# A conv FFN in fp32 halves on one core: down projection by token halves and groups of four inner tiles in the buffers of the up projection, and three plain column pairs instead of two

## The chip, the cores and the metric

The kernel runs on one core of a Trainium2 chip. The metric is the device time of the program in microseconds (us), the median over runs. TensorE (PE in the rows) multiplies, VectorE (DVE), ScalarE (ACT) and GpSimd (POOL) do elementwise work, and SyncE (SP) issues most transfers (DMAs). The granted TensorE clock is shown as a share of full speed: 1.00 is 2.4 GHz, 0.50 is 1.2 GHz.

## The reference, cut to what matters

The program is a whole two-block network on 1024 tokens of width 1024. The change touches its last part alone, the FFN of the second block and the final norm. `h` is the normed input, `x` the residual (`x4` in the kernel, `x` or `x_in` in rows), and there are 2816 = 22 x 128 inner features.

```
def _conv_ffn(h, w_up, conv_w, conv_b, w_down):
    u = _causal_dwconv(h @ w_up, conv_w, conv_b)     # [1024, 2 * 2816], 3 taps along tokens
    a, b = jnp.split(u, 2, axis=-1)
    return (jax.nn.gelu(a) * b) @ w_down
...
        x = x + _conv_ffn(h, f_w_up[l], f_conv_w[l], f_conv_b[l], f_w_down[l])
    return _rmsnorm(x, final_norm_g)
```

## The kernel before, in words

Every fp32 product is made of halves: `split` casts a tile to a rounded high half (ACT, L89) and subtracts it for the low half (VectorE, L92), and `mm3` issues three matmuls for each pair of tiles, high by high (L161), and the two mixed ones (L162, L163). All matmuls of the FFN have 128 x 128 stationary and 128 x 512 moving data.

*Up projection.* It goes over 22 column pairs c, each with one tile of 128 features of `a` and the matching one of `b`, for all 1024 tokens. Right operands are the input's halves in `s.X[0]` and `s.X[1]` (`xghi`, `xglo` in rows), 8 inner tiles each of 512 tokens. The first `first` column pairs run as `plain_pair`: four blocks of 8 inner tiles, 96 matmuls, each block's bank copied out by ACT. The others run as `wino`, a Winograd form: seven products of 4 inner tiles, 84 matmuls, whose banks VectorE sums (L2180). The Winograd right operands are prepared beside the plain columns by `wino_rhs`: `early` writes t1, t2, t3 (tiles `wT1`, `wT2`, `wT3`), one of its eight pieces at each plain block. `late` forms the seventh operand, b12, in four pieces, each by POOL (L2088), VectorE (L2088), POOL (L2109), ACT (L89) and VectorE (L92), and writes it over the first four inner tiles of `s.X[1]`. It is written down after the last plain column, since that column still reads the old contents. The order of the seven right operands is b11, b21, t2, t3, t1, b22, b12: b12 is used by the last product.

Behind the matmuls of a column come the conv (L2216 on ACT, L2218 on VectorE), the gelu, the product of both halves on POOL (L2241, tile `fy`), and a write to DRAM (`gd`, `ffg` in rows; two arrays of 11 feature tiles). The weights of the next column are loaded in tiles `fr` (6 buffers) and turned into Winograd left operands by POOL (L2146 to L2153).

*Down projection.* A pool of its own, `fd`, is opened when the pools `ft` and `ff` of the up projection are closed. For each half n of the 1024 output columns, 22 weight tiles are loaded (L2259) and split; 16 of the 22 go where the input's halves were (so the names `xghi` and `xglo` in rows of the down projection are weights), the others into the pool `wp`; half of the low halves of n = 0 are subtracted on POOL (L2265). Tokens go in pairs of tiles: a tile `fgr` holds 11 feature tiles of 128 tokens (704 KB, L2270), and 33 matmuls run on one bank before the next. Each token tile then gets its x row added (L2290 loads it, on SP; L2291), the sum of squares, and for n = 1 the final norm (L2303) and the store.

*What sets the order.* The calls of the FFN stand in a block whose scheduler orders the instructions of each engine by its own simulation; every engine then works through its list in that order, each instruction waiting for what it needs. Pools hand out their buffers in turn.

Of the kernel before, what the change touches and what calls it, by code (L numbers as in the profile page):

```python
# [10 lines left out]
F32 = mybir.dt.float32  # L11
# [7 lines left out]
P = 128  # L19
D = 1024  # L20
# [23 lines left out]
class Kern:  # L44
# [2148 lines left out]
    def ffn(s, x_in):  # L2193
# [4 lines left out]
        with ExitStack() as es:  # L2198
# [23 lines left out]
            first = 2  # L2222
# [25 lines left out]
        W = I["f_w_down_2"][0]  # L2248
        with ExitStack() as es:
            p = es.enter_context(s.tc.tile_pool(name="fd", bufs=2, reuse_waits="tile"))  # L2250

            slots = [tuple(x[:, k, :] for x in s.X[j]) for j, k in [(0, k) for k in range(8)] + [(1, k) for k in (4, 5, 6, 7, 0, 1, 2, 3)]]

            def weights(n):
                for k in range(NF):
                    at = k - (2, 3)[n]
                    kept = 0 <= at < 16
                    raw = s.t(p, [P, 512], "fdr") if kept else s.t(s.wp, [P, 512], "raw", bufs=3)
                    nc.sync.dma_start(raw, W[k * P : k * P + P, n * 512 : n * 512 + 512])  # L2259
                    if kept:  # L2260
                        h, l = slots[at]
                    else:
                        h, l = (s.t(s.wp, [P, 512], "w" + z, F32R) for z in ("hi", "lo"))
                    nc.scalar.copy(h, raw)
                    (nc.gpsimd if n == 0 and k % 2 else V).tensor_tensor(l, raw, h.bitcast(F32), op=ALU.subtract)  # L2265
                    yield h, l

            def tokens(t, h):
                raw = s.t(p, [P, 11, P], "fgr")
                nc.sync.dma_start(raw, gd[h][:, t * P : t * P + P].rearrange("(k p) t -> p k t", p=P))  # L2270
                g = [s.t(p, [P, 11, P], f"fg{z}", F32R, bufs=4) for z in "hl"]
                s.split(*g, raw)
                return g

            gn, ys, ss = None, [], []
            early = [tokens(t, 0) for t in range(2)]
            for n in range(2):
                cs = slice(n * 512, n * 512 + 512)
                ws = list(weights(n))
                for t2 in range(0, NT, 2):  # L2280
                    o = [s.bank("m") for _ in range(2)]
                    for h in range(2):
# [3 lines left out]
                    for j in range(2):  # L2286
# [11 lines left out]
                        if gn is None:  # L2298
                            gn = s.bcast(p, I["final_norm_g_2"].rearrange("(o d) -> o d", o=1), D, "ffg", bufs=1)
# [236 lines left out]
```

## Time and profile before

| | |
|---|---|
| median of 3 runs | 3416.36 us (3415.32 to 3418.03) |
| the profiled execution, its own time | 3417.99 us |
| its span | 3416.3 us |
| mean granted TensorE clock | 0.975 |
| PE busy | 3203.5 us, 94% of the span |
| VectorE busy | 2207.4 us, 65% |

The profile is of one execution. Busy time of an engine counts its compute instructions; a busy PE can still run at the half clock, which the granted clock of a stretch shows. The up projection ends at 3134.47 us with its last matmul's start, and the down projection fills the rest of the span.

### The profile page before, as it was taken

Reading aid. Unit: us, or ns where it says so; the run is one execution under the profiler, and the core shown is the slowest. Engines: PE = TensorE matmul, PEld = TensorE weight load, DVE = VectorE, ACT = ScalarE, POOL = GpSimd, SP = SyncE. Lnnn points to the kernel's source line nnn. Section 1 sums busy time; section 2 is a strip of 40 time slices with the busy share of each in tenths; the row PEclk is TensorE's granted clock in tenths of the full one; section 3 lists DMA queues with packets and bytes.
Section 4 is the critical chain, followed back from the end, with each engine's and each line's share of the span. In section 5 each row is a group of like instructions: output and inputs, shape, how many; then the busy total and the mean of one; then the engine's idle time right before and its main releaser. Section 6 shows DMA issues by size and latency. Waiting matters only on the chain. (4 is left out here: it accounts for less than half of the span.)

```text
span 3416.3 us, 47135 instructions
## 1 busy us (share of the span) xinstructions
PE 3203.5 (94%) x16605; PEld 2653.7 (78%) x16605; DVE 2207.4 (65%) x4911; ACT 1410.4 (41%) x2863; POOL 737.9 (22%) x964
## 2 busy tenths in 40 slices
PE   7799999999989999998989989999999989998899
PEld 5666689899878788887768777777887778886687
DVE  6676778878855646665686244654445699997342
ACT  5444535445444746652232232332333344443331
POOL 2410021231324000002211011213010464442101
PEclk9999999999999999999999999999999999999999
DMA  7412221111144222215343334434214322224543
GB/s 247 142 56 82 82 65 41 44 50 41 46 150 159 104 73 64 74 59 203 96 110 106 106 107 134 140 117 155 96 56 150 98 68 88 79 90 128 157 140 116
DMA packets 315890, 351.75 MB, mean 103 GB/s; under 512 B 43827, under 2 KB 225007, under 8 KB 315397
## 3 DMA queue, kind: packets, MB, share of 16 engines
q1 hardware_dynamic: 293685, 291.41, 28.1%
q10 hardware_dynamic: 18176, 45.65, 3.6%
q0 software_dynamic: 3792, 11.67, 1.2%
q8 instruction: 131, 2.15, 0.3%
q14 instruction: 106, 0.87, 0.1%
HBM read 262.59 MB, written 86.06 MB: 102 GB/s over the span
## 5 line engine op out<-in xcount | busy, mean ns | idle before, releaser
L161 PE MATMUL pspp<-whi,xghi 128*128 128x512 f32 (+2 forms) x1280 | 453.4, 355 | 15.9 <-DVE hxr L431 8.4
L162 PE MATMUL pspp<-wlo,xghi 128*128 128x512 f32 (+2 forms) x1280 | 443.3, 347 | 1.9 <-DVE wlo L92 1.9
L163 PE MATMUL pspp<-whi,xglo 128*128 128x512 f32 (+2 forms) x1280 | 443.1, 346 | 0.0
L92 DVE TENSOR_TENSOR wlo<-raw,whi 128x512 fp32r<-128x512 f32 (+2 forms) x360 | 257.3, 726 | 150.7 <-ACT whi L89 147.0
L89 ACT CAST whi<-raw 128x512 fp32r<-128x512 f32 (+2 forms) x360 | 213.3, 603 | 265.1 <-DMA raw<-in_w_in 58.5
L161 PEld LDWEIGHTS pspp<-whi,xghi 128*128 128x128 f32 x1280 | 245.2, 192 | 44.2 <-ACT bvh L89 7.9
L163 PEld LDWEIGHTS pspp<-whi,xglo 128*128 128x128 f32 x1280 | 244.7, 191 | 29.1 <-issue 4.2
L162 PEld LDWEIGHTS pspp<-wlo,xghi 128*128 128x128 f32 x1280 | 245.4, 192 | 24.2 <-DVE wlo L92 4.5
L161 PE MATMUL pspp<-whi,oth 128*128 128x512 f32 x512 | 204.7, 400 | 2.3 <-ACT oth L89 1.2
L162 PE MATMUL pspp<-wlo,oth 128*128 128x512 f32 x512 | 201.9, 394 | 0.4 <-DVE wlo L92 0.4
L163 PE MATMUL pspp<-whi,otl 128*128 128x512 f32 x512 | 201.5, 395 | 0.6 <-DVE otl L92 0.5
L161 PE MATMUL pspp<-xghi,whi 128*128 128x512 f32 (+1 forms) x416 | 170.1, 409 | 1.7 <-ACT whi L89 1.2
L163 PE MATMUL pspp<-xghi,wlo 128*128 128x512 f32 (+1 forms) x416 | 167.3, 402 | 0.0
L162 PE MATMUL pspp<-xglo,whi 128*128 128x512 f32 (+1 forms) x416 | 167.3, 402 | 0.0
L162 PE MATMUL psm<-xglo,whi 128*128 128x512 f32 x384 | 152.2, 396 | 5.7 <-DVE xglo L92 5.7
L161 PE MATMUL psm<-xghi,whi 128*128 128x512 f32 x384 | 152.2, 396 | 5.6 <-ACT xghi L89 4.7
L2218 DVE SCALAR_TENSOR_TENSOR fy<-fo,fcw,fy 128x1023 f32<-128x1023 f32 x88 | 143.8, 1652 | 15.1 <-ACT fy L2216 14.2
L163 PE MATMUL psm<-xghi,wlo 128*128 128x512 f32 x384 | 151.3, 394 | 1.3 <-DVE wlo L92 1.3
L92 DVE TENSOR_TENSOR wlo<-fr,whi 128x512 fp32r<-128x512 f32 x106 | 127.6, 1205 | 0.0
L830 DVE TENSOR_SCALAR_CACHE_REDUCE bP<-pss 128x512 f32<-128x512 f32 (+1 forms) x208 | 116.7, 582 | 16.3 <-PE pss L829 15.4
L161 PEld LDWEIGHTS pspp<-whi,oth 128*128 128x128 f32 x512 | 97.0, 189 | 23.6 <-ACT oth L89 2.7
L163 PEld LDWEIGHTS pspp<-whi,otl 128*128 128x128 f32 x512 | 96.8, 189 | 22.4 <-DVE otl L92 1.9
(901 smaller groups left out, 8548.9 us busy)
## 6 DMA issues: line engine op xcount, KB each, us to landing
fgr<-ffg SPq DMA_DIRECT2D x32, 704.0 KB
raw<-in_w_in SPq DMA_DIRECT2D x72, 256.0 KB
fr<-in_f_w_up SPq DMA_DIRECT2D x66, 256.0 KB
raw<-in_adaln_w SPq DMA_DIRECT2D x64, 256.0 KB
x<-ox ACTq DMA_DIRECT2D x32, 512.0 KB
raw<-in_w_out SPq DMA_DIRECT2D x48, 256.0 KB
ox<-x SPq DMA_DIRECT2D x24, 512.0 KB
ffg<-fy ACTq DMA_DIRECT2D x22, 512.0 KB
```

What stands on the lines that cost most here:

```text
L89: i = nc.scalar.copy(hi, src)
L92: return [i.ins, nc.vector.tensor_sub(lo, src, hi.bitcast(F32)).ins]
L161: nc.tensor.matmul(o, ah, bh, start=first and i == 0, stop=False)
L162: nc.tensor.matmul(o, ah, bl, start=False, stop=False)
L163: nc.tensor.matmul(o, al, bh, start=False, stop=last and i == n - 1)
L830: nc.vector.tensor_scalar(Pm[c][:, a - k0 : a - k0 + wd], o[:, :wd], SCALE, None, op0=ALU.mult, op1=ALU.max, accum_out=mx[:, c, n : n + 1])
L2218: V.scalar_tensor_tensor(y[:, 2 - k :], o[:, : SEQ - 2 + k], cw[:, k, f : f + 1], y[:, 2 - k :], op0=ALU.mult, op1=ALU.add)
```

## The change

One more column pair is plain: `first` goes from 2 to 3, and `late` with it moves behind the third column.

The down projection moves into the block in which the pools of the up projection are open, and has no pool of its own. For each half n of the output columns it goes over two halves h of the tokens, with four banks for four token tiles, and over groups of four inner tiles k (the last group has two). A group's features are rows of 128 features by 512 tokens (256 KB) in the `fr` buffers, split into `wT2`, `wT3` and `wT1` in turn. Weight rows are loaded in the same buffers for h = 0 and kept for h = 1. In a group, 12 matmuls run on each of the four banks in turn. The x rows are loaded on POOL's queue (`nc.gpsimd`) into tiles `fo0`, `fo1` and `fy0`, the final norm's gain into `fy1`. All low halves are subtracted on VectorE. The number of matmuls of the down projection and its bytes stay the same.

```diff
@@ -2219,7 +2219,7 @@
                 return y
 
             W = I["f_w_up_2"][0]
-            first = 2
+            first = 3
             load = lambda c: s.wino_load(p, W, (c * P, (NF + c) * P))
             R, early, late = s.wino_rhs(tp, s.X)
             A = []
@@ -2245,49 +2245,49 @@
                         for _ in g:
                             pass
 
-        W = I["f_w_down_2"][0]
-        with ExitStack() as es:
-            p = es.enter_context(s.tc.tile_pool(name="fd", bufs=2, reuse_waits="tile"))
-
-            slots = [tuple(x[:, k, :] for x in s.X[j]) for j, k in [(0, k) for k in range(8)] + [(1, k) for k in (4, 5, 6, 7, 0, 1, 2, 3)]]
-
-            def weights(n):
-                for k in range(NF):
-                    at = k - (2, 3)[n]
-                    kept = 0 <= at < 16
-                    raw = s.t(p, [P, 512], "fdr") if kept else s.t(s.wp, [P, 512], "raw", bufs=3)
-                    nc.sync.dma_start(raw, W[k * P : k * P + P, n * 512 : n * 512 + 512])
-                    if kept:
-                        h, l = slots[at]
-                    else:
-                        h, l = (s.t(s.wp, [P, 512], "w" + z, F32R) for z in ("hi", "lo"))
-                    nc.scalar.copy(h, raw)
-                    (nc.gpsimd if n == 0 and k % 2 else V).tensor_tensor(l, raw, h.bitcast(F32), op=ALU.subtract)
-                    yield h, l
-
-            def tokens(t, h):
-                raw = s.t(p, [P, 11, P], "fgr")
-                nc.sync.dma_start(raw, gd[h][:, t * P : t * P + P].rearrange("(k p) t -> p k t", p=P))
-                g = [s.t(p, [P, 11, P], f"fg{z}", F32R, bufs=4) for z in "hl"]
-                s.split(*g, raw)
-                return g
-
-            gn, ys, ss = None, [], []
-            early = [tokens(t, 0) for t in range(2)]
+
+
+            W = I["f_w_down_2"][0]
+            places = [tuple(x[:, k, :] for x in s.X[j]) for j, k in [(0, k) for k in range(8)] + [(1, k) for k in (4, 5, 6, 7, 0, 1, 2, 3)]]
+
+            def row(src):
+                raw = s.t(p, [P, 512], "fr", bufs=6)
+                nc.sync.dma_start(raw, src)
+                return raw
+
+            def weight(n, k):
+                at = k - (2, 3)[n]
+                raw = row(W[k * P : k * P + P, n * 512 : n * 512 + 512])
+                w = places[at] if 0 <= at < 16 else [s.t(s.wp, [P, 512], "w" + z, F32R) for z in ("hi", "lo")]
+                s.split(*w, raw)
+                return w
+
+            def feature(h, k, o):
+                s.split(*o, row(gd[k // 11][k % 11 * P : k % 11 * P + P, h * 512 : h * 512 + 512]))
+
+            gn, ys, ss, turn = None, [], [], 0
             for n in range(2):
                 cs = slice(n * 512, n * 512 + 512)
-                ws = list(weights(n))
-                for t2 in range(0, NT, 2):
-                    o = [s.bank("m") for _ in range(2)]
-                    for h in range(2):
-                        for j in range(2):
-                            gh, gl = early.pop(0) if early else tokens(t2 + j, h)
-                            s.mm3(o[j], [((gh[:, k, :], gl[:, k, :]), ws[11 * h + k]) for k in range(11)], h == 0, h == 1)
-                    for j in range(2):
-                        t = t2 + j
+                ws = []
+                for h in range(2):
+                    o = [s.bank("m") for _ in range(4)]
+                    for k0 in range(0, NF, 4):
+                        g = [s.t(tp, [P, 4, 512], f"wT{(2, 3, 1)[turn % 3]}{z}", F32R, bufs=1) for z in "hl"]
+                        turn += 1
+                        ks = range(k0, min(k0 + 4, NF))
+                        for k in ks:
+                            if h == 0:
+                                ws.append(weight(n, k))
+                            feature(h, k, [x[:, k - k0, :] for x in g])
+                        for j in range(4):
+                            s.mm3(o[j], [([x[:, k - k0, j * P : j * P + P] for x in g], ws[k]) for k in ks], k0 == 0, k0 + 4 >= NF)
+                    for j in range(4):
+                        t = 4 * h + j
                         ts_ = slice(t * P, t * P + P)
-                        y = s.t(p, [P, 512], f"fx{n}", bufs=(8, 2)[n])
-                        nc.sync.dma_start(y, x_in[ts_, cs])
+                        if t % 2 == 0:
+                            y2 = s.t(p, [P, 2, 512], "fy0" if n else f"fo{h}")
+                        y = y2[:, t % 2]
+                        nc.gpsimd.dma_start(y, x_in[ts_, cs])
                         V.tensor_tensor(y, o[j], y, op=ALU.add)
                         q = s.t(p, [P, 1], f"fss{n}", bufs=(8, 2)[n])
                         nc.scalar.activation(s.t(p, [P, 512], "fj", bufs=1), y, AF.Square, accum_out=q)
@@ -2296,7 +2296,7 @@
                             ss.append(q)
                             continue
                         if gn is None:
-                            gn = s.bcast(p, I["final_norm_g_2"].rearrange("(o d) -> o d", o=1), D, "ffg", bufs=1)
+                            gn = s.bcast(p, I["final_norm_g_2"].rearrange("(o d) -> o d", o=1), D, "fy1")
                         nc.gpsimd.tensor_tensor(q, q, ss[t], op=ALU.add)
                         r = s.rsqrt(p, q, 1, 1.0 / D, "frs")
                         for i, x in enumerate((ys[t], y)):
```

The order of POOL's instructions around `late`, in the kernel before. L2109 forms a piece of b12, L2241 is the product of a finished column, L2146 to L2153 are left operands of the next.

```order
L2088 TENSOR_TENSOR wr_27998<-xghi_26790,xglo_26791 128x512
L2109 TENSOR_TENSOR wr_28000<-wr_28000,wr_27998 128x512
L2088 TENSOR_TENSOR wr_28005<-xghi_26790,xglo_26791 128x512
L2109 TENSOR_TENSOR wr_28007<-wr_28007,wr_28005 128x512
L2088 TENSOR_TENSOR wr_28012<-xghi_26790,xglo_26791 128x512
L2151 TENSOR_TENSOR fr_28026<-raw_28050,fr_28026 128x512
L2153 TENSOR_TENSOR fr_28028<-fr_28028,fr_28026 128x512
L2109 TENSOR_TENSOR wr_28014<-wr_28014,wr_28012 128x512
L2088 TENSOR_TENSOR wr_28019<-xghi_26790,xglo_26791 128x512
L2241 TENSOR_TENSOR fy_27987<-fy_27987,fy_27991 128x1024
L2109 TENSOR_TENSOR wr_28021<-wr_28021,wr_28019 128x512
```

And in the change, from behind the second L2088 of `late`; right ahead of these rows stand its first L2088, a product L2241, its first L2109 and its second L2088.

```order
L2153 TENSOR_TENSOR fr_27983<-fr_27983,fr_27981 128x512
L2146 TENSOR_TENSOR raw_28191<-fr_28171,raw_28173 128x512
L2147 TENSOR_TENSOR fr_28171<-fr_28167,fr_28171 128x512
L2241 TENSOR_TENSOR fy_27970<-fy_27970,fy_27974 128x1024
L2109 TENSOR_TENSOR wr_28148<-wr_28148,wr_28146 128x512
L2088 TENSOR_TENSOR wr_28153<-xghi_26790,xglo_26791 128x512
L2151 TENSOR_TENSOR fr_28167<-raw_28191,fr_28167 128x512
L2153 TENSOR_TENSOR fr_28169<-fr_28169,fr_28167 128x512
L2109 TENSOR_TENSOR wr_28155<-wr_28155,wr_28153 128x512
L2088 TENSOR_TENSOR wr_28160<-xghi_26790,xglo_26791 128x512
L2241 TENSOR_TENSOR fy_28128<-fy_28128,fy_28132 128x1024
L2109 TENSOR_TENSOR wr_28162<-wr_28162,wr_28160 128x512
```

Between the first and the last L2109 stood three instructions that are not of `late`, and now stand seven, two of them products of columns.

SP's list at the start of the down projection, in the kernel before: feature tiles, weights, and then the x rows.

```order
L2270 DMA fgr_31050<-ffg_27591 128x11x128
L2270 DMA fgr_31056<-ffg_27591 128x11x128
L2259 DMA fdr_31074<-in_f_w_down 128x512
L2259 DMA fdr_31078<-in_f_w_down 128x512
L2290 DMA fx_31308<-x_26789 128x512
L2290 DMA fx_31314<-x_26789 128x512
L2290 DMA fx_31478<-x_26789 128x512
L2290 DMA fx_31484<-x_26789 128x512
L2290 DMA fx_31648<-x_26789 128x512
L2290 DMA fx_31654<-x_26789 128x512
L2290 DMA fx_31818<-x_26789 128x512
L2290 DMA fx_31824<-x_26789 128x512
```

And in the change, behind the last two loads of the up projection: rows `fr` of weights and features in turn.

```order
L2124 DMA fr_30772<-in_f_w_up 128x4x128
L2124 DMA raw_30774<-in_f_w_up 128x4x128
L2255 DMA fr_31039<-in_f_w_down 128x512
L2255 DMA fr_31045<-ffg_27591 128x512
L2255 DMA fr_31049<-in_f_w_down 128x512
L2255 DMA fr_31055<-ffg_27591 128x512
L2255 DMA fr_31059<-in_f_w_down 128x512
L2255 DMA fr_31063<-ffg_27591 128x512
L2255 DMA fr_31067<-in_f_w_down 128x512
L2255 DMA fr_31071<-ffg_27591 128x512
```

The x rows have left the list, and no load here is larger than 256 KB.

The last instructions of VectorE in the kernel before: the sums L2291 and the products L2303 of the last token tiles, and ahead of them the last feature subtraction (L92).

```order
L92 TENSOR_TENSOR fgl_32612<-fgr_32609,fgh_32611 128x1408
L2303 SCALAR_TENSOR_TENSOR fx_31654<-fx_31654,frs_32483,ffg_32094 128x512
L2303 SCALAR_TENSOR_TENSOR fx_32476<-fx_32476,frs_32483,ffg_32094 128x512
L2291 TENSOR_TENSOR fx_32648<-psm_32490,fx_32648 128x512
L2303 SCALAR_TENSOR_TENSOR fx_31818<-fx_31818,frs_32655,ffg_32094 128x512
L2303 SCALAR_TENSOR_TENSOR fx_32648<-fx_32648,frs_32655,ffg_32094 128x512
L2291 TENSOR_TENSOR fx_32662<-psm_32491,fx_32662 128x512
L2303 SCALAR_TENSOR_TENSOR fx_31824<-fx_31824,frs_32669,ffg_32094 128x512
L2303 SCALAR_TENSOR_TENSOR fx_32662<-fx_32662,frs_32669,ffg_32094 128x512
```

And in the change, for the last four token tiles.

```order
L2291 TENSOR_TENSOR fy_32805<-psm_32437,fy_32805 128x512
L2291 TENSOR_TENSOR fy_32805<-psm_32438,fy_32805 128x512
L2303 SCALAR_TENSOR_TENSOR fo_31891<-fo_31891,frs_32812,fy_32387 128x512
L2303 SCALAR_TENSOR_TENSOR fy_32805<-fy_32805,frs_32812,fy_32387 128x512
L2291 TENSOR_TENSOR fy_32832<-psm_32439,fy_32832 128x512
L2303 SCALAR_TENSOR_TENSOR fo_31891<-fo_31891,frs_32825,fy_32387 128x512
L2303 SCALAR_TENSOR_TENSOR fy_32805<-fy_32805,frs_32825,fy_32387 128x512
L2291 TENSOR_TENSOR fy_32832<-psm_32440,fy_32832 128x512
L2303 SCALAR_TENSOR_TENSOR fo_31902<-fo_31902,frs_32839,fy_32387 128x512
L2303 SCALAR_TENSOR_TENSOR fy_32832<-fy_32832,frs_32839,fy_32387 128x512
L2303 SCALAR_TENSOR_TENSOR fo_31902<-fo_31902,frs_32852,fy_32387 128x512
L2303 SCALAR_TENSOR_TENSOR fy_32832<-fy_32832,frs_32852,fy_32387 128x512
```

Four token tiles now end behind the last group's splits, and the sums of the third and fourth stand behind products of the first and second.

## Rows read from the trace of the kernel before

**Rows 1.** The page: span, and busy time with share and instructions of each engine.

```profile
span 3416.3 us, 47135 instructions
...
PE 3203.5 (94%) x16605; PEld 2653.7 (78%) x16605; DVE 2207.4 (65%) x4911; ACT 1410.4 (41%) x2863; POOL 737.9 (22%) x964
```

**Rows 2.** Windows: stretch, length, busy time (instructions) by engine, PEclk, DMA share, GB/s.

```profile
core 0: us, PE busy (x) PEld busy (x) DVE busy (x) ACT busy (x) POOL busy (x), PEclk, DMA share, GB/s
2757.00:2776.00 19.00, 8.69 (x23) 5.56 (x22) 18.29 (x18) 5.50 (x9) 11.39 (x8) 0.64 0.27 83
3050.00:3100.00 50.00, 50.00 (x222) 41.42 (x221) 47.02 (x50) 21.55 (x29) 22.67 (x14) 1.00 0.24 74
3134.70:3187.00 52.30, 25.45 (x78) 16.81 (x78) 19.75 (x17) 17.20 (x20) 9.53 (x6) 0.74 0.72 223
3190.00:3390.00 200.00, 200.00 (x884) 165.62 (x883) 73.90 (x73) 57.54 (x77) 14.90 (x20) 1.00 0.46 141
```

**Rows 3.** Timeline of PE, 2756 to 2777: start, duration, instruction, [idle before <-releaser].

```profile
2755.71 0.39 PE L163 MATMUL psm<-xghi,wlo 128*128 128x512 f32 x1
...
2757.07 0.39 PE L163 MATMUL psm<-xghi,wlo 128*128 128x512 f32 x1
...
2765.18 0.80 PE L162 MATMUL psm<-xglo,whi 128*128 128x512 f32 x1 [4.64 <-DVE xglo L92]
...
2774.94 0.40 PE L161 MATMUL psm<-xghi,whi 128*128 128x512 f32 x1
```

**Rows 4.** Timeline of ACT, POOL and VectorE (DVE), 2742 to 2771.

```profile
2744.99 0.62 ACT L89 CAST xghi<-wr 128x512 fp32r<-128x512 f32 x1 [2.12 <-POOL wr L2109]
...
2757.10 2.24 POOL L2109 TENSOR_TENSOR wr<-wr,wr 128x512 f32<-128x512 f32 x1
2759.43 1.60 POOL L2088 TENSOR_TENSOR wr<-xghi,xglo 128x512 f32<-128x512 f32 x1
2762.24 2.34 POOL L2241 TENSOR_TENSOR fy<-fy,fy 128x1024 f32<-128x1024 f32 x1 [1.22 <-DVE fy L2218]
2766.50 1.26 POOL L2109 TENSOR_TENSOR wr<-wr,wr 128x512 f32<-128x512 f32 x1 [1.92 <-DVE wr L2088]
...
2768.84 1.38 DVE L92 TENSOR_TENSOR xglo<-wr,xghi 128x512 fp32r<-128x512 f32 x1
```

**Rows 5.** Timeline of PE, 3133 to 3190, the start of the down projection.

```profile
3134.47 0.39 PE L163 MATMUL psm<-xghi,wlo 128*128 128x512 f32 x1
3144.81 0.80 PE L161 MATMUL psm<-whi,fgh 128*128 128x512 f32 x1 [9.96 <-ACT fgh L89]
...
3166.38 1.22 PE L161 MATMUL psm<-xghi,fgh 128*128 128x512 f32 x2 [12.90 <-ACT xghi L2264]
...
3184.86 0.51 PE L161 MATMUL psm<-whi,fgh 128*128 128x512 f32 x1 [0.53 <-ACT fgh L89]
```

**Rows 6.** Timeline of all engines, 3408 to 3417, the end of the kernel.

```profile
3408.72 0.39 PE L163 MATMUL psm<-whi,fgl 128*128 128x512 f32 x1
3409.14 0.69 DVE L2291 TENSOR_TENSOR fx<-psm,fx 128x512 f32<-128x512 f32 x1 [3.32 <-PE psm L163]
...
3411.88 1.42 DVE L2303 SCALAR_TENSOR_TENSOR fx<-fx,frs,ffg 128x512 f32<-128x512 f32 x2 [2.05 <-POOL frs L171]
```

**Rows 7.** Timeline of SP, 3135 to 3160: time that SP spent on issuing.

```profile
3141.62 11.02 SPq L2290 DMA_DIRECT2D fx<-x  x9
```

**Rows 8.** The chain of waits, 3134 to 3187: start, us, what.

```profile
3143.03 6.90 DMA ffg<-fy
...
3155.69 8.72 DMA fgr<-ffg
...
3169.16 3.70 DMA fdr<-in_f_w_down
...
3180.41 2.49 DMA fdr<-in_f_w_down
```

**Rows 9.** Groups of instructions, 3134.7 to 3417: count, busy us, mean ns, idle before.

```profile
L92 DVE TENSOR_TENSOR fgl<-fgr,fgh 128x1408 fp32r<-128x1408 f32 x32 | 51.9, 1625 | 67.0 <-ACT fgh L89 66.9
```

**Rows 10.** Groups of instructions of POOL, 1700 to 1900.

```profile
L1474 POOL DMA_DIRECT2D s5CA<-s5CA x16 | 10.1, 630 | 53.9 <-DVE s5z L1386 43.7 <-DVE wlo L92 10.2
```

## The prediction, made before the changed kernel was timed

> **What bounds the kernel now.** I read the page first: TensorE is busy 94% of the span [rows 1], so an edit pays only where TensorE stands still or runs at its half clock; what the other engines lose elsewhere is free. Then I read the stretches around the edit as windows. In the middle of both products TensorE never stops: 50.00 of 50 us in the up projection, 200.00 of 200 us in the down projection, granted clock 1.00 in both [rows 2]. There a matmul follows the last one every 1.36/6 = 0.2267 us (the six steps from 2755.71 to 2757.07, [rows 3]). Two stretches are different [rows 2]: 2757 to 2776 has PE busy 8.69 of 19.00 us at clock 0.64, 3134.7 to 3187 has it busy 25.45 of 52.30 us at 0.74. The timelines say why.
>
> *Stall A, first Winograd column.* From the matmul at 2757.07 to the one at 2774.94 there are 16 steps in 17.87 us [rows 3]; at 0.2267 they are 3.63 us, so 14.2 us are lost. The reader should see the releaser, xglo from VectorE, 4.64 us at one matmul: product 6 multiplies with b12, and its four pieces come late. ACT writes the first at 2744.99; the last subtraction on POOL runs at 2766.50, and VectorE ends the last xglo at 2768.84 + 1.38 = 2770.22 [rows 4]: 25.2 us from first to last, because every piece queues behind the column work on POOL (its product fy, 2.34 us at 2762.24, is one such row) and on VectorE, which is busy 18.29 of the 19.00 us [rows 2].
>
> *Stall B, start of the down projection.* The last up matmul starts at 3134.47; the first down matmul waits 9.96 us for a feature tile, another 12.90 us for a weight, and the last small wait is at 3184.86 [rows 5]. There are 22 × 3 × 8 × 2 = 1056 down matmuls by the code, so the last would start 1056 × 0.2267 = 239.4 us after the last up matmul, at 3373.9, if nothing waited. It starts at 3408.72 [rows 6]: 34.9 us lost. SP's row shows the start of it: nine x_in loads hold SP 11.02 us from 3141.62 [rows 7], ahead of further features and weights, and the chain shows what they wait for, the landing of the last up column's write (6.90 us from 3143.03); behind it come a 704 KB feature load (8.72 us) and weight loads with two buffers, 3.70 and 2.49 us each [rows 8].
>
> **The change, part by part.**
>
> 1. *One more plain column.* 96 matmuls instead of 84: 12 × 0.2267 = **+2.7 us**, on the path, since TensorE sets the pace there. A plain column's bank copies go to ACT instead of sums to VectorE, which makes VectorE's queue shorter there.
>
> 2. *Stall A.* Column c=2 starts 77 matmuls before 2757.07, at 2739.6. As a plain column it ends 96 matmuls later, at 2761.4; product 6 of c=3 starts 72 later at 2777.7, and needs the fourth b12 piece after nine more, at 2779.7. But c=2 now still reads the old contents of that place: its fourth block reads piece 0 at matmuls 73 to 75, so the first b12 piece can be written from 2756.6, not from 2745. If the chain again takes 25.2 us, the last piece ends at 2781.8, 2.1 us late. By POOL's new order (shown above) it is shorter: the second L2109 can run when ACT and VectorE have finished piece 0, at about 2760; then L2109, L2088, L2151 and L2153, by rows of such subtractions (1.60 for L2088, 1.26 to 2.24 for L2109, [rows 4]) some 7 us; the third L2109 at about 2767; L2088, the product fy (2.34) and the fourth L2109 to about 2774.5; ACT (0.62) and VectorE (1.38) to 2776.5, or 3 us later if VectorE is as full as before. That is in time. Bounds: nothing lost, or 2.1 us; I take half, **+1.0 us**. So A gives **−14.2**, of which 1.0 comes back.
>
> 3. *Stall B.* SP's list no longer has x_in loads or 704 KB tiles: behind the last up loads come rows of 256 KB, weight and feature in turn, in six buffers that the up projection already owns. So the first group needs no closed pool: its feature splits go to wT2, free after product 2 of the last column, 48 matmuls or 10.9 us before the up matmuls end; wT3 and wT1 come free 2.7 and 5.4 us after. Group 0 has eight rows, eight casts on ACT and eight subtractions on VectorE at about 0.6 to 0.7 us (0.62 for the cast of [rows 4]; 1.625 × 512/1408 = 0.59 by the subtraction of 1408 columns, [rows 9]): some 5.6 us, done about 5 us before it is needed. Each further group has 48 matmuls, 10.9 us, for its eight rows: 2.10 MB in 10.9 us, 193 GB/s. The start before moved 223 GB/s over 52 us [rows 2], and did so with two buffers for weights. After group 0 the need per group is the same until the token half is done (264 matmuls, 59.8 us); the second half loads features only. Bounds: nothing gained (TensorE waits for the loads as long as now), or all 34.9 us. I take all, **−34.9 us**, because group 0 is early and the rate fits.
>
> 4. *x_in on the POOL queue.* Sixteen loads that POOL issues; such a DMA, of another tile, held POOL 0.63 us earlier in the kernel [rows 10], 10 us in all on an engine that is busy 14.90 of 200 us in the down projection [rows 2]. Each is wanted only when four banks end, 59.8 us after the half began; nothing on the path. If they were late by some us, the banks would still be free: eight exist, four are in use. **0**, bounds 0 and +1.
>
> 5. *The subtractions.* All on VectorE now: 88 + 44 at 0.7 us, 92 us over 239 us, where 32 × 1.625 us [rows 9] and the weights' stood before. VectorE was busy 73.90 of 200 us [rows 2]: hidden. **0**.
>
> 6. *The tail.* Now one token tile ends last: its bank is done with the matmul at 3408.72, the sum (0.69) runs on VectorE at 3409.14, the last two products (1.42) at 3411.88 [rows 6], 4.6 us in all. In the change four tiles end within 18 matmuls (4.1 us), in the last group of two inner tiles, and VectorE does for them four sums and eight products in one queue, in the order shown above: 4 × 0.69 + 8 × 0.71 = 8.4 us. Walking down that order with the delay of 3411.88 − 3409.83 = 2.05 us from a sum to its products, the last product ends 6.6 us after the last matmul starts: **+2.1 us** (0 to +4).
>
> Sum: 2.7 − 14.2 + 1.0 − 34.9 + 2.1 = **−43.3 us**. The profiled execution took 3417.99 us (span 3416.3, [rows 1]), 1.6 above the median of 3416.36; taken from the median this gives **3373 us**. With no residue and no longer tail it is 3370; with 2.1 us of residue, 1 us for x_in and 4 us of tail 3377.
>
> **The rivals.**
>
> *B12 again (chance 0.10).* The wait of stall A comes back at c=3 as a whole. For it: the place comes free 12 us later than it was used before, VectorE is full, and there are more foreign rows between the four L2109 on POOL. Against: 16 us more until product 6. Price: 14.2 − 1.0 = 13.2 us, so 3386.
>
> *First groups late (0.10).* Groups 1 to 3 stall by 10 to 15 us in sum, since the last up column's write, the up loads and the row loads meet in the same transfers (6.90 us for that write, [rows 8]). TensorE would then drop to its half clock too, as it did at the start before (0.74 in the mean, [rows 2]). Price about 13, so 3386.
>
> *Loads that cannot feed (0.05), the other side.* SP issues in order, and a row waits for one of six buffers; each buffer is held from issue to its subtraction. If one load in effect follows another, 44 loads at 2.49 us [rows 8] are 109.6 us against the 59.8 us of a half; with two such halves that is 2 × 49.8 = 99.6 us lost, 3473. It decides from 21.6 us a half, (59.8 + 21.6)/44 = 1.85 us a load, 142 GB/s. Against: 223 GB/s seen. The Trainium skill speaks for this one: "SBUF — State Buffer", section "The DMA setup-cost knee", says every transfer pays about 2 us beside its bytes, and advises the largest single transfer; its fit would give 2.6 us for 256 KB, an estimate from that page that agrees with the 2.49 us here. By the rule the change, which cuts 704 KB into 256 KB, would lose unless several loads are under way.
>
> *Bank by bank (0.03).* TensorE now changes the bank every 12 matmuls instead of 33; a pause at each change would hold the clock down. Against: the up projection also changes every 12 and has no gap in 50 us [rows 2]. If each of the 96 runs on a bank cost two steps more, 0.45 us, that is 43 us, and 3416: no change. The Trainium skill names such a case, "TensorE: Matmul & The Clock Gate", section "A second HAM failure mode: psum-queue depth-cycling": cycling through banks brings short idles and an oscillating clock. The 50 us of this trace disagree.
>
> *The change does not do it (0.02).* The group order is not kept and the waits merely move: 3416.
>
> **How the numbers follow.** The likeliest case has 0.70: 3373, own range 3368 to 3379. Range for 8 in 10: 3368 to 3388, which takes in the two rivals at 3386. This kernel's runs lie within 0.1%, so 0.2% (6.8 us) is about what can be told from no change. Faster: 0.70 + 0.10 + 0.10, less a little for their tails: 0.89. Same: 0.03 + 0.02 = 0.05. Slower: 0.06.
>
> **What would show it.** Up: no wait over 1 us at product 6 of c=3, granted clock 1.00 through 2757 to 2785; a wait for xghi or xglo of L2109's pieces there would show step 2 wrong. Down: the first down matmul within 1 us of the last up matmul, PE busy throughout the first 60 us; a wait for a cast whose own releaser is a row load would show step 3 wrong, at group 1 to 3 the second rival, in every group of both first halves the third. Tail: 6.6 us from the last matmul's start to the last product. The prediction fails above all if the row loads, in order and in six buffers, don't run several at a time.

## The result, and the profile after

The changed kernel takes 3373.02 us (median of 4 runs, 3368.76 to 3380.61) beside 3416.05 us for the kernel before (4 runs): a ratio of 0.9876, 95% interval 0.9857 to 0.9894. The forecast was 3373 us, in a range of 3368 to 3388. The profiled execution is the run of 3368.76 us.

The page of the changed kernel, its span and busy times (for [rows 1]):

```profile
span 3367.1 us, 47405 instructions
...
PE 3186.9 (95%) x16617; PEld 2645.2 (79%) x16617; DVE 2201.6 (65%) x4968; ACT 1416.0 (42%) x2919; POOL 724.0 (22%) x965
```

The start of the down projection (for [rows 5]), timeline of PE: the last up matmul and the first down matmul.

```profile
3117.46 0.39 PE L163 MATMUL psm<-xghi,wlo 128*128 128x512 f32 x1
3117.69 0.39 PE L161 MATMUL psm<-whi,wT2h 128*128 128x512 f32 x1
```

No bracket stands behind the second: 0.23 us after the last up matmul the first down matmul starts. The last one starts at 3356.82, and 3117.69 + 1055 × 0.22667 = 3356.82: nothing is lost in the whole down projection. Windows of the change, the first Winograd column, the first token half and most of the rest (for [rows 2]):

```profile
2768.00:2777.00 9.00, 5.30 (x16) 3.72 (x15) 9.00 (x11) 2.18 (x4) 4.15 (x3) 0.81 0.36 116
3118.00:3180.00 62.00, 62.00 (x275) 51.35 (x274) 36.69 (x54) 29.81 (x53) 6.51 (x7) 1.00 0.69 227
3180.00:3350.00 170.00, 170.00 (x751) 140.77 (x750) 59.77 (x94) 48.56 (x95) 8.42 (x16) 1.00 0.42 133
```

PE is full at clock 1.00 in the last two. The first is what is left of stall A, here as a timeline of PE (for [rows 3]):

```profile
2768.48 0.39 PE L163 MATMUL psm<-xghi,wlo 128*128 128x512 f32 x1
2771.26 0.50 PE L161 MATMUL psm<-xghi,whi 128*128 128x512 f32 x1 [2.39 <-ACT xghi L89]
2773.07 0.79 PE L162 MATMUL psm<-xglo,whi 128*128 128x512 f32 x1 [1.30 <-DVE xglo L92]
```

Two waits, 4.1 us from start to start beyond the usual step, and eight steps at a lower clock behind them, 1.4 us: 5.6 us lost, where the forecast left 1.0. The tail (for [rows 6]), the last matmul and VectorE's last product, with one of POOL's small steps between:

```profile
3356.82 0.39 PE L163 MATMUL psm<-whi,wT1l 128*128 128x512 f32 x1
...
3358.86 0.67 POOL L2300 TENSOR_TENSOR fss<-fss,fss 128x1 f32<-128x1 f32 x1 [0.83 <-DVE fo L2303]
...
3363.28 0.75 DVE L2303 SCALAR_TENSOR_TENSOR fy<-fy,frs,fy 128x512 f32<-128x512 f32 x1
```

From here on the measure is the FFN stretch: from the first up matmul (2691.14 us before, 2681.34 in the change) to the end of the span. It is 725.1 us before and 685.7 in the change, −39.4. What runs ahead of it is the same code; in the fourteen profiles of this study the first up matmul starts between 2680.8 and 2691.1, so ten us of a total say nothing of an edit in the FFN. Each row of the table below is one profiled execution; x_on_sp, three_bufs, half_loads, token_quarters, half_runs, own_pool, three_raw and before_x_pool were run once.

Losses are worked out from the starts of the FFN's matmuls: a stretch of n steps loses its length less n × 0.22667 us. "Start" is the first 100 steps, "A" the rest of the up projection, "B" from the last up matmul to the last down matmul, "tail" from there to the end.

| kernel | start | A | B | tail | FFN stretch |
|---|---|---|---|---|---|
| before | 4.95 | 14.28 | 34.89 | 7.57 | 725.1 |
| the change | 3.73 | 5.58 | 0.00 | 10.23 | 685.7 |
| plain3_only | 4.81 | 3.07 | 34.46 | 7.56 | 716.1 |
| down_only | 3.68 | 15.86 | 0.00 | 10.21 | 693.2 |
| blocks_turned | 3.67 | 0.00 | 0.00 | 10.21 | 680.1 |
| x_on_sp | 4.97 | 2.96 | 0.00 | 10.20 | 684.3 |
| three_bufs | 3.89 | 5.56 | 0.00 | 10.22 | 685.8 |
| half_loads | 3.74 | 5.57 | 0.00 | 11.08 | 686.6 |
| token_quarters | 5.01 | 2.90 | 3.99 | 8.38 | 686.5 |
| half_runs | 5.06 | 2.90 | 0.00 | 10.21 | 684.4 |
| own_pool | 4.73 | 3.18 | 17.33 | 10.18 | 701.6 |
| three_raw | 4.70 | 3.19 | 6.51 | 10.32 | 690.9 |
| before_x_pool | 5.07 | 14.21 | 30.69 | 7.58 | 721.0 |
| turned_and_staggered | 4.79 | 0.00 | 0.00 | 7.61 | 678.6 |

### The profile page after: what moved, and what is told of

It reads as the page before. It is cut to its first block, busy times and chain, and to the rows that moved or that the text cites. A ratio compares the mean times of both kernels' runs of the same rounds, so it can differ in the third digit from the quotient of the medians.

```text
span 3367.1 us, 47405 instructions
## 1 busy us (share of the span) xinstructions
PE 3186.9 (95%) x16617; PEld 2645.2 (79%) x16617; DVE 2201.6 (65%) x4968; ACT 1416.0 (42%) x2919; POOL 724.0 (22%) x965
## 3 DMA queue, kind: packets, MB, share of 16 engines
q0 software_dynamic: 5072, 15.86, 1.6%
## 5 line engine op out<-in xcount | busy, mean ns | idle before, releaser
L92 DVE TENSOR_TENSOR wlo<-raw,whi 128x512 fp32r<-128x512 f32 (+2 forms) x359 | 253.6, 718 | 149.0 <-ACT whi L89 143.2
L92 DVE TENSOR_TENSOR wlo<-fr,whi 128x512 fp32r<-128x512 f32 x116 | 130.8, 1129 | 14.6 <-ACT whi L89 14.6
```

The lines of the kernel that those rows point to most:

```text
L92: return [i.ins, nc.vector.tensor_sub(lo, src, hi.bitcast(F32)).ins]
```

## The experiments

**The two parts alone.** plain3_only is the kernel before with

```diff
-            first = 2
+            first = 3
```

> Measure: the FFN stretch, from the first up matmul to the end of the span (725.2 us before, 685.8 in the change, so -39.4). Here only the third plain column pair is added to the kernel before. Theory (the parts are independent): the wait at the first Winograd column shrinks from 14.2 to the 5.6 us that the change shows, 12 matmuls cost 2.7, the start of the down projection stays as it was (34.9 lost): 725.2 - 8.6 + 2.7 = 719.3 us. Rival 1 (my step 2 was right and the 5.6 us come from the down projection's rows in the same block): about 1 us is left, 714.7 us. Rival 2 (the wait only moves by a column): 14.2 us stay, 727.9 us.

Measured: 716.1 us, between theory and the first rival; 3406.9 us in total, ratio 0.9978 (0.9969 to 0.9987). Timeline of PE, first Winograd column and start of the down projection:

```profile
2776.99 0.50 PE L161 MATMUL psm<-xghi,whi 128*128 128x512 f32 x1 [1.23 <-ACT xghi L89]
2778.79 0.50 PE L162 MATMUL psm<-xglo,whi 128*128 128x512 f32 x1 [1.30 <-DVE xglo L92]
...
3132.19 0.79 PE L161 MATMUL psm<-whi,fgh 128*128 128x512 f32 x1 [9.95 <-ACT fgh L89]
...
3153.41 1.22 PE L161 MATMUL psm<-xghi,fgh 128*128 128x512 f32 x2 [11.85 <-ACT xghi L2264]
```

The wait at product 6 is there without the new down projection, so it belongs to the plain column's part; the waits of the start are those of [rows 5]. The loss of A comes in two sizes, 2.9 to 3.2 and 5.6, and goes with the start: where the first 100 steps lose 4.7 us or more it is 3, where they lose 3.7 to 3.9 it is 5.6. The matmul that needs the last xglo starts 91.6 to 91.7 us after the first up matmul in the change (2773.07 − 2681.34) as in plain3_only (2778.79 − 2687.16): b12 comes when it comes, and TensorE reaches it sooner or later. That is 1.2 us of the difference. The rest is the clock behind the waits; here are 8 us from the last matmul ahead of them, in plain3_only and in the change:

```profile
2775.30:2783.30 8.00, 5.47 (x24) 3.99 (x23) 8.00 (x10) 2.61 (x5) 3.88 (x3) 1.00 0.27 74
```
```profile
2768.40:2776.40 8.00, 4.30 (x13) 2.90 (x12) 8.00 (x10) 2.18 (x4) 4.15 (x3) 0.79 0.32 102
```

The granted clock stays at 1.00 in the first and falls in the second, to 0.50 between 2772.6 and 2775.9. The two sizes of the start are the clock's too: it is 0.50 for the first 5.8 us in the change and for the first 8.1 us in plain3_only.

down_only is the change with `first = 2`.

> Only the new down projection, with two plain column pairs as before. Theory: the start of the down projection loses nothing (-34.9), the tail is 2.7 us longer, the wait at the first Winograd column is as before, 14.2 us: FFN stretch 725.2 - 34.9 + 2.7 = 693.0 us. Rival: with one block for both projections the order around the first Winograd column changes too, and its wait with it: below 688 or above 698 us.

Measured: 693.2 us, as the theory says, though A is 15.86 where the theory has 14.2 and the start loses 1.3 less; 3385.0 us in total, ratio 0.9915 (0.9898 to 0.9931). Timeline of PE at the first Winograd column, and a window of the down projection:

```profile
2764.43 0.79 PE L162 MATMUL psm<-xglo,whi 128*128 128x512 f32 x1 [4.35 <-DVE xglo L92]
```
```profile
3140.00:3340.00 200.00, 200.00 (x884) 165.62 (x883) 91.37 (x139) 72.77 (x138) 14.91 (x23) 1.00 0.54 175
```

The parts are nearly independent: −31.9 and −9.1 us make −41.0, with −39.4 for both. Of the 1.6 left 1.1 lie in the start and A, whose sizes change from run to run, and 0.4 in B of plain3_only.

**Why A was not closed.** blocks_turned is the change with

```diff
-        for n, (i, j) in enumerate(((0, 0), (1, 0), (0, 1), (1, 1))):
+        for n, (i, j) in enumerate(((0, 1), (1, 1), (0, 0), (1, 0))):
```

> The change, with the four blocks of a plain column in another order: the two that read the tile over which b12 is written come first. So the first b12 piece may be written about 10.9 us (48 matmuls) earlier. Theory (the place of b12 comes free too late, and the chain of four pieces then takes some 24 us): the 5.6 us of wait go, FFN stretch 685.8 - 5.6 = 680.2 us. Rival (VectorE's queue of column work is full and its order holds the pieces, whenever the place is free): the last piece ends within 2 us of where it does, 684 to 686 us.

Measured: 680.1 us, the theory's number; 3369.51 us in total, ratio 0.9871 (0.9853 to 0.9889). Its window at the first Winograd column, and VectorE's last xglo:

```profile
2765.00:2785.00 20.00, 20.00 (x90) 16.56 (x89) 18.69 (x19) 8.21 (x13) 10.20 (x6) 1.00 0.26 79
```
```profile
2764.39 0.68 DVE L92 TENSOR_TENSOR xglo<-wr,xghi 128x512 fp32r<-128x512 f32 x1
```

The last piece ends 77.6 us after the first up matmul (2764.39 + 0.68 − 2687.51), in the change 91.7. The chain was not only moved forward but is shorter too: 18.4 us from its first cast at 2746.65, against 24.5 in the change, where it falls into a stretch that keeps VectorE busy for 24.26 of the 24.47 us (14.32 of 18.42 in blocks_turned). That shows the rival partly right about the cause, and the place of b12 as what decides. The change's timeline of ACT and VectorE shows the queue:

```profile
2748.55 0.63 ACT L89 CAST xghi<-wr 128x512 fp32r<-128x512 f32 x1
...
2760.83 1.77 DVE L92 TENSOR_TENSOR wlo<-fr,whi 128x512 fp32r<-128x512 f32 x1
2762.53 2.32 DVE L2218 SCALAR_TENSOR_TENSOR fy<-fo,fcw,fy 128x1022 f32<-128x1022 f32 x1
2764.77 0.67 DVE L2180 TENSOR_TENSOR fo<-fo,psm 128x512 f32<-128x512 f32 x1
2765.37 2.55 DVE L92 TENSOR_TENSOR xglo<-wr,xghi 128x512 fp32r<-128x512 f32 x1
...
2771.63 1.39 DVE L92 TENSOR_TENSOR xglo<-wr,xghi 128x512 fp32r<-128x512 f32 x1
```

The third xglo could run at 2762.7, when ACT had cast its piece, and stands behind the conv and a sum until 2765.37.

**What removed the 34.9 us at the start.** These runs change one property each. own_pool closes the pools of the up projection first:

```diff
+            es.close()
+            tp = p = es.enter_context(s.tc.tile_pool(name="fd", bufs=2, reuse_waits="tile"))
```

> The change, but the pools of the up projection are closed ahead of the down projection, whose tiles then come from one pool of its own, in the same loops and sizes. Theory (a new pool's tiles lie where tiles of the up projection lie, and come free only with the end of its last column's work, so nothing is loaded ahead): TensorE waits 5 to 15 us at the switch and again at the next groups, FFN stretch 692 to 706 us. Rival (loops and rows alone removed the stall, wherever the tiles lie): 684 to 688 us.

Measured: 701.6 us; 17.3 of the 34.9 us are back. Timelines of SP, ACT and PE, and the chain:

```profile
3114.34 0.35 SPq L2257 DMA_DIRECT2D fr<-in_f_w_down  x1
```
```profile
3125.01 1.06 ACT L2240 ACTIVATE fy<-fy 128x1024 f32<-128x1024 f32 x1
3130.23 0.33 ACTq L2242 DMA_DIRECT2D ffg<-fy  x1
3130.60 0.62 ACT L89 CAST whi<-fr 128x512 fp32r<-128x512 f32 x1 [4.54 <-POOL fy L2241]
3131.12 0.61 ACT L89 CAST wT2h<-fr 128x512 fp32r<-128x512 f32 x1
```
```profile
3131.79 2.07 PE L161 MATMUL psm<-whi,wT2h 128*128 128x512 f32 x4 [9.32 <-ACT wT2h L89]
3146.14 0.79 PE L161 MATMUL psm<-xghi,wT2h 128*128 128x512 f32 x1 [4.08 <-ACT wT2h L89]
```
```profile
3134.69 10.77 DMA fr<-ffg
```

The first six rows were issued from 3114.34 on, before the last up matmul (3122.08), and the first had landed at 3117.07 by the trace's semaphore updates. But their casts stand in ACT's list behind all work of the last column, down to its write (L2242), which waits for POOL's product. In the change ACT's list has them mixed with the last two columns. ACT there, the four casts to wT2, the write of column 20, then, with more casts between, conv and write of column 21:

```profile
3107.01 2.19 ACT L89 CAST wT2h<-fr 128x512 fp32r<-128x512 f32 x4 [1.32 <-PE psm L163]
3109.16 0.33 ACTq L2242 DMA_DIRECT2D ffg<-fy  x1
...
3120.10 1.25 ACT L2216 ACTIVATE fy<-fo,fcw 128x1024 f32<-128x1024 f32 x1 [1.19 <-DVE fo L2180]
...
3134.61 0.33 ACTq L2242 DMA_DIRECT2D ffg<-fy  x1
```

Group 0 is cast ahead of the last column's conv, as soon as TensorE lets go of wT2 (the wait of 1.32 us for PE). That is what the open pools give: 9.5 us at the switch, and 7.8 us behind it, because the next rows then all start at once and land late (10.77 us). The open pools also let the first row go out 41 us earlier, counted from the first up matmul (3067.17 in the change); what each of the two is worth is not shown. The other 17.6 of the 34.9 us are gained with closed pools too, by the new loops and rows.

token_quarters uses four token quarters with two banks:

```diff
-                for h in range(2):
-                    o = [s.bank("m") for _ in range(4)]
+                for h in range(4):
+                    o = [s.bank("m") for _ in range(2)]
```

> The change, with four quarters of the tokens (two banks each) in place of two halves; features are rows of 128 KB, weights are loaded in the first quarter. The bytes are the same, but the first quarter wants 22 weights and 22 half rows, 8.65 MB, in 132 matmuls or 29.9 us: 289 GB/s in place of 193. The kernel before wanted as much (22 weights and four feature tiles in 132 matmuls). Theory (what removed the wait at the start is that the weights are spread over twice as many matmuls): at 226 GB/s the 8.65 MB take 38 us, of which some 5 are loaded ahead; TensorE waits 3 to 6 us in the first quarter, the tail is 1 to 1.5 us shorter, FFN stretch 687 to 691 us. Rival (the rate does not matter; loading ahead in open pools and in small rows removed it): 684 to 685 us.

Measured: 686.5 us, 4.0 us lost in the first quarter, the tail 1.9 shorter. Timeline of PE and the window of the first quarter:

```profile
3148.45 0.49 PE L161 MATMUL psm<-xghi,wT3h 128*128 128x512 f32 x1 [2.50 <-ACT wT3h L89]
```
```profile
3124.50:3158.00 33.50, 30.47 (x132) 24.22 (x131) 25.11 (x44) 18.99 (x38) 6.87 (x7) 1.00 0.85 270
```

At twice the weights in the same time TensorE waits again, at 270 GB/s. The theory holds, for 4 us of the 34.9; the stretch lies 0.5 us below its range, since A has its smaller size here.

three_bufs and three_raw ask for the buffers.

```diff
+                s.t(p, [P, 512], "fr", bufs=6)
                 raw = s.t(p, [P, 512], "fr", bufs=6)
```

> The change, with every second of the six buffers left unused in the down projection, so that three loads at most are under way or waiting for their split. In the change the loads of the first token half follow each other 1.16 us apart (226 GB/s) and group 1 is split 4.7 us before it is needed. Theory (several loads under way are what feeds the first halves): a buffer is held some 5 us from issue to subtraction, so 1.7 us a load against the 1.36 that are needed; TensorE waits 5 to 20 us over the two first halves, FFN stretch 690 to 706 us. Rival (the order of the rows alone does it, two or three buffers are enough): 684 to 686 us.

Measured: 685.8 us. But a tile that nothing touches got no buffer: SP issues the first 29 rows within 0.4 us of the times of the change, counted from the first up matmul. All six were still in use, so the run says nothing on the question, and is a repeat of the change. In its place three_raw has

```diff
-                raw = s.t(p, [P, 512], "fr", bufs=6)
+                raw = s.t(s.wp, [P, 512], "raw", bufs=3)
```

> Three buffers in earnest: in the run meant for it the six buffers were all still in use. Here the rows of the down projection go to the three buffers of another tile of the same size. Theory (several loads under way feed the first halves): a buffer is held some 5 us, so 1.7 us a load against 1.36 needed; TensorE waits 5 to 20 us in the first halves, FFN stretch 690 to 706 us. Rival (three are enough): 684 to 687 us.

Measured: 690.9 us, 6.5 lost in four waits of 1.1 to 2.1 us, with the short ones right behind them, in the first token half and none in the second of the halves that load weights:

```profile
3138.43 0.50 PE L161 MATMUL psm<-xghi,wT3h 128*128 128x512 f32 x1 [1.34 <-ACT wT3h L89]
...
3150.66 0.50 PE L161 MATMUL psm<-xghi,wT1h 128*128 128x512 f32 x1 [1.22 <-ACT wT1h L89]
```

The theory's lower end. Six buffers feed at 1.16 us a row (from SP's issue at 3123.95 to that at 3148.22 in the change are 21 rows), three at 1.63 (32 rows from 3124.27 to 3176.37), where 1.36 are needed.

before_x_pool is the kernel before with its x loads on POOL's queue:

```diff
-                        nc.sync.dma_start(y, x_in[ts_, cs])
+                        nc.gpsimd.dma_start(y, x_in[ts_, cs])
```

> The kernel before with one edit, its x loads on POOL's queue, so that SP goes on to features and weights 11 us earlier. Theory (of the 34.9 us at the start of the down projection, those in which SP stood on the x loads come back): 8 to 12 us, FFN stretch 713 to 717 us. Rival (features and weights wait for their own buffers and for 286 GB/s that the first 30 us ask for, whatever SP does): 722 to 726 us.

Measured: 721.0 us, 4.2 gained at the start, between the two. Timelines of ACT and PE, and the chain:

```profile
3132.70 0.33 ACTq L2242 DMA_DIRECT2D ffg<-fy  x1
3133.07 2.63 ACT L89 CAST fgh<-fgr 128x1408 fp32r<-128x1408 f32 x2 [4.33 <-POOL fy L2241]
```
```profile
3134.49 0.80 PE L161 MATMUL psm<-whi,fgh 128*128 128x512 f32 x1 [9.95 <-ACT fgh L89]
...
3151.80 1.22 PE L161 MATMUL psm<-xghi,fgh 128*128 128x512 f32 x2 [8.58 <-ACT xghi L2264]
```
```profile
3138.61 11.23 DMA fgr<-ffg
```

The first wait stays. The first feature tile is issued 2.7 us after the last up matmul in both kernels and had landed at 3131.34 here, by the semaphore updates; its cast stands behind the last column's write, as in own_pool, but that holds it back only 1.7 us, and its late issue and its landing make the rest of this wait. The second shrinks from 12.90 to 8.58: its tile is issued 14.5 us after the last up matmul instead of 21.2, but lands in 11.23 us instead of 8.72, probably because the 704 KB tiles now start together (0.5 us apart, 2.5 before).

x_on_sp puts the x loads of the change back on SP.

> The change, with the sixteen x loads on SP's queue as before, not on POOL's. In SP's list the first four of them then stand behind ten rows of the down projection, and write tiles that the last up column's conv still reads. Theory (SP stands still until that conv is done, some 6 us after the last up matmul, and the rows behind are late): TensorE waits 1 to 6 us at the second group, FFN stretch 687 to 692 us. Rival (the queue does not matter, since the new order of the loads alone removed the stall): 685 to 686.5 us.

Measured: 684.3 us, 0.7 below the rival's range since A has its smaller size; B is 0.00, as the rival says. SP's own timeline shows why the theory fell:

```profile
3109.49 3.68 SPq L2290 DMA_DIRECT2D fo<-x  x4
```

The four loads held SP 3.68 us, not to the end of the last conv, and group 1 has that much in hand (4.7 us in the change). In the new order POOL's queue buys nothing.

**Small sizes.** half_loads loads each row by two transfers, half_runs changes the bank every six matmuls.

```diff
-                nc.sync.dma_start(raw, src)
+                for i in (0, 256):
+                    nc.sync.dma_start(raw[:, i : i + 256], src[:, i : i + 256])
```

> The change, with each row of 256 KB loaded by two transfers of 128 KB. Theory (SP issues one in 0.6 us at best, so 1.2 us a row against 1.36 needed, and a transfer's fixed part lies beside the others under way): margins get smaller, no wait of more than 1 us, FFN stretch 684.5 to 688 us. Rival (each transfer's fixed time adds up): more than 1.85 us a row, both first halves wait, over 700 us.

```diff
-                        for j in range(4):
-                            s.mm3(o[j], [([x[:, k - k0, j * P : j * P + P] for x in g], ws[k]) for k in ks], k0 == 0, k0 + 4 >= NF)
+                        for ks in (ks[:2], ks[2:]):
+                            for j in range(4):
+                                if ks:
+                                    s.mm3(o[j], [([x[:, k - k0, j * P : j * P + P] for x in g], ws[k]) for k in ks], ks[0] == 0, ks[-1] == NF - 1)
```

> The change, with six matmuls on a bank before the next in place of twelve: 176 changes of bank in place of 96. Theory (a change of bank costs TensorE nothing): FFN stretch 685 to 687 us, granted clock 1.00 throughout the down projection. Rival (each change costs a short idle, and the clock follows): 80 more changes by 0.1 to 0.45 us, 694 to 722 us.

Measured: 686.6 and 684.4 us, B 0.00 in both. half_loads lies in its theory's range, with 0.9 us more behind VectorE's last product, and SP issues the halves of a row 0.42 us apart in the median, not 0.6 at best; half_runs lies 0.6 below its own, with the smaller A. Windows of the first token half of half_loads, then of half_runs:

```profile
3122.00:3184.00 62.00, 62.00 (x275) 51.38 (x274) 37.58 (x54) 31.25 (x54) 5.90 (x7) 1.00 0.71 225
```
```profile
3121.00:3183.00 62.00, 62.00 (x275) 51.35 (x274) 36.61 (x54) 29.73 (x53) 6.50 (x7) 1.00 0.67 223
```

Transfers of 128 KB move 225 GB/s, as those of 256 KB do (227 in the change, 223 in half_runs). The Trainium skill ("SBUF — State Buffer", section "The DMA setup-cost knee") lets the rate fall with the size of a transfer. Here, with several under way, both sizes feed all that the stretch asks for; what either could move at most is not shown. The bank changes cost nothing at half the run length either, so the short idles of "TensorE: Matmul & The Clock Gate", section "A second HAM failure mode: psum-queue depth-cycling" (the same skill) don't appear in this trace.

**A version that joins what the runs point to.** turned_and_staggered is blocks_turned with the last two groups of the last token half bank by bank:

```diff
+                        held.append((g, k0, ks))
+                        if n == h == 1 and k0 == 16:
+                            continue
                         for j in range(4):
-                            s.mm3(o[j], [([x[:, k - k0, j * P : j * P + P] for x in g], ws[k]) for k in ks], k0 == 0, k0 + 4 >= NF)
+                            for g, k0, ks in held:
+                                s.mm3(o[j], [([x[:, k - k0, j * P : j * P + P] for x in g], ws[k]) for k in ks], k0 == 0, k0 + 4 >= NF)
+                        held = []
```

> The change with the blocks of a plain column turned (no wait at the first Winograd column, 680.05 us) and, in the last token half of all, the matmuls of the last two groups (six inner tiles) bank by bank: 18 on each bank, so that the four token tiles end 4.1 us apart in place of 1.4. Theory (the tail of 10.2 us is four sums and eight products of VectorE in one queue behind ends that lie too close): the last tile alone is left at the end, 7.6 to 8.2 us from the last matmul's start to the end, FFN stretch 677.4 to 678.1 us. Rival (the tail is the last tile's own chain through ACT, POOL and VectorE, as long as before): 680 us.

Measured: 678.6 us, the tail 7.61; 3368.06 us in total (3365.79 to 3369.62), ratio 0.9866 (0.9850 to 0.9882). Timeline of the end:

```profile
3358.99 0.39 PE L163 MATMUL psm<-whi,wT1l 128*128 128x512 f32 x1
3359.42 0.69 DVE L2296 TENSOR_TENSOR fy<-psm,fy 128x512 f32<-128x512 f32 x1
...
3362.83 0.74 DVE L2308 SCALAR_TENSOR_TENSOR fy<-fy,frs,fy 128x512 f32<-128x512 f32 x1
```

The tail is the theory's; the stretch lies 0.5 us above its range, since the start loses 1.1 more than in blocks_turned. One tile alone is left at the end, as before the change. By the FFN stretch it beats the change by 7.1 us; by the totals alone, whose intervals overlap, it could not be told from it.

## Why the prediction was right

The sum was −43.3 us; the FFN gave −39.4, the median of the totals −43.0. The rest, 3.6 us, lies ahead of the FFN in code that is the same, within the spread there, so that the median came out at the forecast is partly chance.

1. *One more plain column*, +2.7: as forecast, by the count.
2. *Stall A.* Forecast to give 13.2 of 14.2; it gave 8.7 in the profiled execution (14.28 − 5.58). This is the mis-sized term: half of 2.1 us was taken for the residue, and it is 5.6 (2.9 to 5.6 over the runs). The bound of 2.1 failed twice. The chain was as long as the bound took it (24.5 us, forecast 25.2), but its first cast ran not when the place was free but some 3 us later, behind column work on ACT (2768.48 is the 81st matmul of c=3, and the last matmul that reads piece 0 gives way to the next 101 steps ahead of it, at 2745.6; the cast is at 2748.55), so that the two waits make 4.1 us; and the price of the wait left out the steps at the lower clock behind it, 1.4 us. The walk down POOL's order, which said 2776.5, counted VectorE's durations but not its queue. blocks_turned shows the place of b12 to be what decides: free 48 matmuls earlier, it leaves no wait.
3. *Stall B*, −34.9: exactly so, 34.89 to 0.00. The reason was named in part. Group 0 is early as forecast: its casts to wT2 begin when that comes free, at 3107.01, 10.7 us before the first down matmul (forecast 10.9). What was not named is that they must also stand ahead of the last column's work in ACT's list, as they do with the pools open (own_pool, 17.3 us). The rate of 193 GB/s (token_quarters, 4.0) and the six buffers (three_raw, 6.5) are each needed. These three don't add up to a division of the 34.9, as each was taken away alone. That x_in loads on SP were a main cause was wrong: 4.2 us of 34.9 in the kernel before, and nothing in the new order.
4. *x_in on POOL's queue* and 5. *the subtractions*: 0, as forecast.
6. *The tail*: forecast +2.1, measured 2.66 (10.23 − 7.57): the last product ends 7.2 us after the last matmul's start, not 6.6. From the end of the last sum to its products it is 2.52 us, where the walk took 2.05, as one of POOL's small steps there (L170) takes 0.58 us and took 0.19 at the end of the kernel before.

Not forecast is the start, 1.2 us less lost in this execution (4.95 to 3.73); the two sizes come and go over the runs, with A moving the other way. With it the sum is 2.7 − 8.7 − 34.9 + 2.7 − 1.2 = −39.4.

Of the rivals, b12 came back by a third of its price, and none of the others appeared: the loads ran 1.16 us apart, far from the 1.85 that decides.

## What to carry to other kernels

When a phase begins with a stall, look not only at its loads but at where its first casts stand in the list of the engine that also finishes the phase before: keeping the pools open let the scheduler put them ahead, and closing them alone brought back half of that stall. A buffer that is overwritten late should be read first: turning the order of four blocks took away the rest of stall A, 5.6 us, without one more matmul. Whether it would have done so with two plain column pairs, without the third, was not run. Where a gain is no larger than the spread of what runs ahead of its stage, compare the stretch in the profiles, not the totals.

## What was not expected of the hardware

What a wait costs hangs on the clock behind it: waits of 2.39 and 1.30 us cost 5.6, with the granted clock at 0.50 for the steps behind them, and waits of 1.23 and 1.30 us cost 3.1, with the clock at 1.00 (plain3_only). A start slower by 1.3 us made the later loss 2.7 us smaller, so that the FFN came out 1.4 us shorter (half_runs against the change, 684.4 and 685.7). Of the 2.7, 1.3 come from the wait being for work that didn't depend on TensorE, the rest from the clock, which stayed at 1.00 in half_runs.

POOL's steps of one column (L2300, L170) took 0.19 us alone or beside VectorE's sums L2291. Beside its products of 128 × 512 (L2303) they took up to 0.67: of those behind the last four tiles, each that began beside a product ended 0.05 us after it. In the kernel before, L2300 took 1.01 us beside a subtraction of 1408 columns.
